# Pairing the sample batches in the indexer and attention part of a hybrid-layer decode kernel

## The chip, the cores and the metric

The kernel runs on one core of a Trainium2 chip. The metric is device microseconds of one execution, as the median of three runs.

## The reference

One layer of a hybrid decoder: two mixers read the same input projection, and their outputs are merged. There are 256 prompt tokens and 8 sample sequences ("batches") of 8 new tokens, each with 1024 cached positions, so 320 tokens in all. Mixer A is a gated delta rule (GDN) with a matrix state per head. Mixer B is sparse attention: an indexer scores the keys, the best are selected, and attention runs over those. The sample part of mixer B, which the change touches, computes:

```python
kidx_all = concatenate([cache_kidx[page_table], kidx])                 # 1024 + 8 keys per batch
logits = einsum('bqhd,bkd->bqhk', qi, kidx_all) * IDX_DH ** -0.5       # 16 indexer heads
score = einsum('bqhk,bqh->bqk', relu(logits), wi) * IDX_HEADS ** -0.5
idx = top_k(score, 256)
s = einsum('bqngd,bqknd->bqngk', q, k_sel) * ATT_DH ** -0.5            # 2 KV heads, 8 query heads each
o = einsum('bqngk,bqknd->bqngd', softmax(s), v_sel)
```

Each of these products exists once per batch, with 8 tokens; all weights' products are over the 320 tokens together.

## The kernel before

A Python planner writes the whole program out once, in order. `Kernel.stream` (L387) is its spine: 480 units, each of which loads 512 KB of weights (`raw`), casts them on ScalarE (`whi`), subtracts on VectorE (`wlo`), and multiplies with 24 main matmuls of 128 weight columns against the 320 tokens (16 of `whi` with the high and low parts of the tokens, 8 of `wlo`). Casts and differences are written two units ahead. After the 12th and the 24th matmul of a unit `side_round` (L305) lets every waiting side generator take one step, if the planner's clock says that its operands are ready (`ready`, `until`, `need`, `idle`). Matmuls of the generators so stand between main matmuls; a few generators must come first for the stream to go on, and then `force` (L329) runs side rounds with no main matmul between them. Below, "main count" is the number of main matmuls that stand ahead of a place in TensorE's queue.

Side generators that the change or its effects touch:

- `aux_gen` (L1114): products of the small columns (index weights, decay and beta), among the first side work.
- `sample_branch` (L1411): for one batch after another it gathers the indexer keys (`a8` tiles, 1024 + 1024 columns: as gathered and transposed in 32 by 32 blocks on VectorE), multiplies them with the queries `qiS` (16 matmuls in four row groups, one PSUM bank each, with 256 of the bank's 512 columns used), applies the relu, and in the next turn sums over heads with `wsel` (4 matmuls and one of 8 columns for the new keys). The queries come back from DRAM per batch into two slots (`fill`, L1388). The rows go to `scs`, where 32 rounds on VectorE select the best. `gate_gen` (L862) shares the `a8` ring.
- Its second half is the attention: per batch a gather of K and one of V (1 MB each), 32 by 32 transposes of K on VectorE, a visit with the mask products (`bs`, `esel`) and the scores (`qS`), reductions and five exponentials, a visit with 36 transposes of the probabilities (`tr4`, L242), and a visit with the value sums. `sample_out` (L1610) turns a batch's output and multiplies it with the gate.
- GDN, from main count 3744: `v_done` (L1795) takes a `vf` tile for each value block and forces side rounds until one is free. A tile becomes free in `v_gen` (L2055), when the value block is turned, and a `vt` tile to turn it into is free only after `prompt_chain` (L2086) and `sample_chain` (L2163) of an earlier head pair have finished. Before these stands `inverse` (L1938), the triangular inverse of the chunks, in parts.

Side products use six PSUM banks (`ps`), main ones two (`pm`). Helpers record every operation, so all rows of the profile carry line L64.

## Time and profile before

| | us |
|---|---|
| median of three runs (2122.76 to 2122.95) | 2122.89 |
| the profiled execution, its own time | 2128.34 |
| its span, first to last instruction | 2126.6 |
| TensorE busy in the span | 2093.1 |
| VectorE busy | 1416.3 |
| ScalarE busy | 985.3 |
| GpSimd busy | 464.0 |

The clock that TensorE was granted is 0.998 of full speed over the span. In a timeline each row has the start, the length, the engine, the operation with its output and inputs, and the count of instructions that the row groups; a bracket gives the idle time ahead of it and what ended it. TensorE's matmuls of four-byte numbers leave two records each. Lengths overlap, so what a piece of work takes on TensorE is read from start to start.

### The profile page before, as it was taken

How to read it: one execution, taken by the hardware profiler on the slowest of the kernel's cores; microseconds unless marked ns; L12 is line 12 of the kernel's file. 1: busy time of each engine (PE TensorE's matmuls, PEld its weight loads, DVE VectorE, ACT ScalarE, POOL GpSimd, SP SyncE). 2: the span in 40 equal slices, each digit the busy share in tenths (PEclk: the TensorE clock that was granted, in tenths of full speed). 3: DMA queues.
4: the chain of work that ended last, by engine and by line, in shares of the span. 5: the costliest groups of instructions: out<-in, count | busy, mean ns of one | idle time of the engine just before them, and what ended most of it. 6: DMA issues, size and time to landing. Idle time of an engine off the chain costs nothing.

```text
span 2126.6 us, 45305 instructions
## 1 busy us (share of the span) xinstructions
PE 2093.1 (98%) x17769; PEld 2020.2 (95%) x17769; DVE 1416.3 (67%) x2898; ACT 985.3 (46%) x2253; POOL 464.0 (22%) x661
## 2 busy tenths in 40 slices
PE   7999999999999999999999999999999999999997
PEld 7999989999999999899999999999999999999997
DVE  4776647889855477777878786868665545455543
ACT  3224473333344455465646464656545534333343
POOL 1001000000010108361818181818080000000000
PEclk9999999999999999999999999999999999999999
DMA  9996659776578667686868686868687867555562
GB/s 344 333 337 184 177 140 261 224 210 197 167 239 247 202 186 203 160 233 181 228 173 232 173 232 171 234 170 229 171 245 214 247 204 211 169 154 150 163 181 81
DMA packets 713989, 438.99 MB, mean 206 GB/s; under 512 B 73936, under 2 KB 697136, under 8 KB 711472
## 3 DMA queue, kind: packets, MB, share of 16 engines
q1 hardware_dynamic: 709696, 413.45, 68.3%
q0 software_dynamic: 3616, 21.02, 3.0%
q8 instruction: 139, 2.28, 0.5%
q10 hardware_dynamic: 464, 1.65, 0.2%
q14 instruction: 74, 0.61, 0.1%
HBM read 386.81 MB, written 48.94 MB: 205 GB/s over the span
## 4 chain that ended last, share of the span: by engine, by line
PE 70%; issue 22%; DVE 3%; DMA 2%; ACT 2%; SPq 0%; DVEq 0%; POOL 0%; POOLq 0%; ACTq 0%
PE pm L64 54%; PE ps L64 16%; DVE S L64 1%; DVE wlo L64 1%; DMA rawx<-in_w_ada_dram 1%; DMA a<-in_w_ada_dram 1%; DMA out_dram<-s 0%; DVE ps L64 0%; ACT whi L64 0%; DMA qiS<-d_qi 0%; ACT ot L64 0%; SPq L64 0%; DMA c<-in_c_sample_dram 0%; ACT s L64 0%; DMA cst<-in_state_conv_dram 0%
## 5 line engine op out<-in xcount | busy, mean ns | idle before, releaser
L64 PE MATMUL pm<-xh,whi 128*128 128x320 f32 (+1 forms) x3108 | 942.5, 317 | 2.7 <-DVE qiS L64 1.3
L64 PE MATMUL pm<-xl,whi 128*128 128x320 f32 (+1 forms) x3108 | 910.2, 307 | 0.3 <-DVE xl L64 0.2
L64 DVE TENSOR_TENSOR wlo<-raw,whi 128x1024 fp32r<-128x1024 f32 x466 | 576.8, 1247 | 245.8 <-ACT whi L64 233.7
L64 PEld LDWEIGHTS pm<-xh,whi 128*128 128x128 f32 x3108 | 584.2, 188 | 27.9 <-issue 20.2
L64 PEld LDWEIGHTS pm<-xl,whi 128*128 128x128 f32 x3108 | 585.0, 188 | 1.6 <-DVE xl L64 0.7
L64 ACT ACTIVATE whi<-raw 128x1024 fp32r<-128x1024 f32 x466 | 488.5, 1058 | 168.1 <-PE pm L64 103.8
L64 PE MATMUL pm<-xh,wlo 128*128 128x320 f32 (+1 forms) x3108 | 521.3, 307 | 0.5 <-DVE wlo L64 0.5
L64 PEld LDWEIGHTS pm<-xh,wlo 128*128 128x128 f32 x3108 | 469.4, 188 | 0.9 <-DVE wlo L64 0.9
L64 POOL TENSOR_TENSOR X<-X,tmpx 48x31 f32<-48x31 f32 (+15 forms) x248 | 175.5, 708 | 19.4
L64 POOL TENSOR_TENSOR tmpx<-blk,X 48x31 f32<-48x31 f32 (+15 forms) x248 | 162.0, 653 | 53.0 <-DMA blk<-d_b 34.8
L64 DVE SCALAR_TENSOR_TENSOR ps<-xp,cs,ps 128x344 f32<-128x344 f32 x192 | 111.5, 581 | 6.8
L64 POOL TENSOR_TENSOR sc<-sc,mh 128x6 f32<-128x6 f32 (+1 forms) x24 | 44.3, 1848 | 285.4 <-DVE sc L64 206.0
L64 PE MATMUL pm<-y1h,whi 128*128 128x320 f32 x336 | 99.5, 309 | 1.8 <-DVE M L64 0.9
L64 POOL TENSOR_TENSOR rfin<-rfin,mh 128x3 f32<-128x3 f32 x1 | 0.8, 848 | 455.5 <-DVE rfin L64 455.5
L64 PE MATMUL pm<-y1l,whi 128*128 128x320 f32 x336 | 99.1, 307 | 0.0
L64 DVE SCALAR_TENSOR_TENSOR S<-S,gtr,ps 128x128 f32<-128x128 f32 x256 | 67.4, 342 | 0.1
L64 PEld LDWEIGHTS pm<-y1h,whi 128*128 128x128 f32 x336 | 62.8, 187 | 2.3 <-ACT whi L64 2.3
L64 PE MATMUL ps<-xh,whi 128*128 128x320 f32 (+1 forms) x220 | 64.7, 309 | 0.0
L64 ACT ACTIVATE xp<-pm 128x256 f32<-128x256 f32 (+1 forms) x128 | 32.0, 304 | 70.5 <-PE pm L64 70.5
L64 ACT ACTIVATE ot<-ot,sc 128x128 f32<-128x128 f32 x96 | 29.9, 390 | 73.5 <-DVE sc L64 73.5
L64 PE MATMUL ps<-xl,whi 128*128 128x320 f32 (+1 forms) x220 | 63.7, 304 | 0.0
L64 PEld LDWEIGHTS pm<-y1l,whi 128*128 128x128 f32 x336 | 63.1, 188 | 0.0
(403 smaller groups left out, 2793.3 us busy)
## 6 DMA issues: line engine op xcount, KB each, us to landing
raw<-in_w_in_dram SPq DMA_DIRECT2D x328, 512.0 KB
raw<-in_w_pa_dram SPq DMA_DIRECT2D x64, 512.0 KB
rawx<-in_w_ada_dram SPq DMA_DIRECT2D x18, 1024.0 KB
a<-in_w_ada_dram SPq DMA_DIRECT2D x16, 1024.0 KB
S<-in_state_gdn_dram SPq DMA_DIRECT2D x32, 512.0 KB
out_dram<-S SPq DMA_DIRECT2D x32, 512.0 KB
raw<-in_w_pb_dram SPq DMA_DIRECT2D x32, 512.0 KB
raw<-in_w_out_dram SPq DMA_DIRECT2D x32, 512.0 KB
```

Of the source, the lines that this page charges most:

```text
L64: made = fn(*args, **kw)
```

## The change

The sample branch handles batches in pairs. Two batches' scores share a PSUM bank (256 columns each), in the indexer and in the attention; the head sums of two batches stand together, with `wsel` padded from 8 to 32 columns so that a whole 32-row group is copied out at once; the sums for the new keys are made once for all eight batches (`put_own`). In the attention the transposes of two batches stand in one visit (64 small ones and one of 128 by 128 for the own scores), and so do the value sums of two batches. The eight tiles of a ring that is no longer used become a fourth `a8` tile, and the five `s` tiles the transposed probabilities. K and V of the first batches are asked for at round 24 of the selection if the gate generator has finished. New waits stand ahead of the matmuls of `aux_gen`, and some `ready` times have 1.5 or 2.0 us added.

```diff
+        self.flags.add("gate")
...
-        self.q_r = Ring([a.tile([128, NP], F32, name=f"q{j}") for j in range(EARLY)])
+        self.qall = a.tile([128, EARLY * NP], F32, name="qall")
+        self.q_r = Ring([self.qall[:, NP * j:NP * j + NP] for j in range(EARLY)])
...
-        self.wsel = a.tile([128, NB, TS], F32, name="wsel")
+        self.wsel = a.tile([128, NB, 32], F32, name="wsel")
...
-        self.s_r = Ring([a.tile([128, 384], F32, name=f"s{j}") for j in range(5)])
+        self.sall = a.tile([128, 2048], F32, name="sall")
+        self.s_r = Ring([self.sall[:, 384 * j:384 * j + 384] for j in range(5)])
...
-        self.a4 = Ring([a.tile([128, 9, 128], F32, name=f"a4{j}") for j in range(2)])
-        self.st = Ring([a.tile([128, 8], F32, name=f"st{j}") for j in range(6)])
+        self.a4 = Ring([a.tile([128, 2, 1024], F32, name="a4")])
+        self.st = Ring([a.tile([128, 16], F32, name=f"st{j}") for j in range(6)])
+        self.own2 = a.tile([128, 256], F32, name="own2")
+        self.own, self.ownT = self.own2[:, 0:128], self.own2[:, 128:256]
+        self.vSo = a.tile([128, 256], F32, name="vSo")
...
     def aux_gen(self):
         nc, a, i = self.nc, self.ap, self.i
         ax = self.auxf
+        yield self.ready(ax)
+        yield from self.need(self.ps_side)
...
-        yield
+        yield self.ready(g, rb)
+        yield from self.need(self.ps_side, 2)
...
-        yield
+        yield self.ready(self.G)
+        yield from self.need(self.ps_side)
...
+            self.nc.sync.dma_start(self.vSo[64:128, 128 * n:128 * n + 128], self.vS[0:64, 128 * n:128 * n + 128])
...
+        def turned(b):
+            yield from self.until(self.ready(raws[b][:, 0:1024]) + 1.5)
+            turn(raws[b][:, 1024:2048], raws[b][:, 0:1024])
...
-        for b in range(NB + 1):
-            yield from self.need(self.ps_side, (4 if b < NB else 0) + (b > 0))
...
+        for b in range(0, NB + 2, 2):
+            while b > 2 and not {f"s{b - 4}", f"s{b - 3}"} <= self.flags:
+                yield
+            yield from self.need(self.ps_side, (4 if b < NB else 0) + (b > 0) + (b == 2))
             if b > 0:
-                yield from self.need(self.s_r)
+                if b == 2:
+                    yield from self.need(self.s_r)
                 p = self.psum()
-                for g in range(4):
-                    self.mm(p[32 * g:32 * g + 8, 0:256], self.wsel[:, b - 1, :],
-                            last.rearrange("p a b -> p (a b)")[:, 256 * g:256 * g + 256], skip=True)
-                self.mm(p[0:8, 256:264], self.wsel[:, b - 1, :], self.newi[:, b - 1, :], skip=True)
+                for e in range(2):
+                    for g in range(4):
+                        self.mm(p[32 * g:32 * g + 32, 256 * e:256 * e + 256], self.wsel[:, b - 2 + e, :],
+                                last[:, e, 256 * g:256 * g + 256], skip=True)
+                if b == 2:
+                    pn = self.psum()
+                    for c in range(NB):
+                        self.mm(pn[0:32, 8 * c:8 * c + 8], self.wsel[:, c, :], self.newi[:, c, :], skip=True)
                 self.a4.put(last)
             if b < NB:
                 last = self.a4.get()
-                rl = last.rearrange("p a b -> p (a b)")
                 ps = [self.psum() for _ in range(4)]
-                kt = raws[b][:, 1024:2048].rearrange("p (e j c) -> p j e c", e=8, j=4)
-                q = self.slot(self.qiS, b)
-                for j in range(4):
-                    for g in range(4):
-                        r = slice(32 * g, 32 * g + 32)
-                        self.mm(ps[g][:, 0:256].rearrange("p (e c) -> p e c", e=8), q[r, j, :], kt[r, j],
-                                start=(j == 0), stop=(j == 3), skip=True)
+                for e in range(2):
+                    kt = raws[b + e][:, 1024:2048].rearrange("p (e j c) -> p j e c", e=8, j=4)
+                    q = self.slot(self.qiS, b + e)
+                    for j in range(4):
+                        for g in range(4):
+                            r = slice(32 * g, 32 * g + 32)
+                            self.mm(ps[g][:, 256 * e:256 * e + 256].rearrange("p (e c) -> p e c", e=8), q[r, j, :], kt[r, j],
+                                    start=(j == 0), stop=(j == 3), skip=True)
                 for g in range(4):
-                    self.act(rl[:, 256 * g:256 * g + 256], ps[g][:, 0:256], AF.Relu, scale=SC)
+                    self.act(last[:, :, 256 * g:256 * g + 256], ps[g].rearrange("p (e c) -> p e c", e=2), AF.Relu, scale=SC)
                     self.ps_side.put(ps[g])
-                self.a8.put(raws.pop(b))
+                for e in range(2):
+                    self.a8.put(raws.pop(b + e))
             if b > 0:
+                for e in range(2):
+                    sb = sums[e]
+                    self.act(sb.rearrange("r (c e) -> r e c", e=8),
+                             p[:, 256 * e:256 * e + 256].rearrange("r (e c) -> r e c", e=8))
+                    self.spawn(put_scores(b - 2 + e, sb))
+                self.ps_side.put(p)
+            if b == 2:
                 sb = self.s_r.get()
-                for g in range(4):
-                    r = slice(32 * g, 32 * g + 8)
-                    self.act(sb[r, 0:256].rearrange("r (c e) -> r e c", e=8),
-                             p[r, 0:256].rearrange("r (e c) -> r e c", e=8))
-                self.act(sb[0:8, 248 + 8 * b:256 + 8 * b], p[0:8, 256:264])
-                self.ps_side.put(p)
-                self.spawn(put_scores(b - 1, sb))
-            if b + 3 < NB:
-                yield from fetch(b + 3)
-            if b + 1 < NB:
-                yield from self.until(self.ready(raws[b + 1]))
-                turn(raws[b + 1][:, 1024:2048], raws[b + 1][:, 0:1024])
+                self.act(sb[0:32, 0:64], pn[0:32, 0:64])
+                self.ps_side.put(pn)
+                self.spawn(put_own(sb))
+            yield from fetch(b + 3)
+            yield from fetch(b + 4)
             if b + 2 < NB:
-                yield self.idle(self.slot(self.qiS, b))
-                self.fill(self.qiS, self.d_qi, b + 2)
-            if b + 1 < NB:
-                yield from self.until(self.ready(raws[b + 1], self.slot(self.qiS, b + 1), last))
+                yield from turned(b + 2)
+                yield self.idle(self.qiS[:, 0:8])
+                for e in range(2):
+                    self.fill(self.qiS, self.d_qi, b + 2 + e)
+                yield from turned(b + 3)
+                yield max(self.ready(raws[b + 2], raws[b + 3], last), self.ready(self.qiS[:, 0:8]) + 2.0)
...
+            if it == 24 and "gate" in self.flags:
+                for b in range(2):
+                    yield from load(K, ck, b)
+                yield from load(V, cv, 0)
...
+            yield from self.until(self.ready(K[b]) + 1.5)
...
+        self.q_r.free.clear()
+        self.s_r.free.clear()
+        self.a8.put(self.qall)
+        yield from load(V, cv, 1)
+        pT = self.sall.rearrange("p (k r) -> p k r", r=128)
+        own, ownT = self.own, self.ownT
+        vown = self.vS, self.vSo
+        width = (256, 256, 256, 256, 64)
+        order = (4, 0, 1, 2, 3)
+        for b in range(0, NB, 2):
+            yield self.ready(K[b], K[b + 1], self.bs, self.qS)
...
-            ktv = K[b].rearrange("p (e n j c) -> p n j e c", e=8, n=2, j=4)
-            qr = self.slot(self.qS, b)
-            es = self.esel[:, b % 4].rearrange("p h t -> p (h t)")
-            width = (256, 256, 256, 256, 64)
-            for g, (p, w) in enumerate(zip(ps, width)):
-                k, c = (slice(32 * g, 32 * g + 32), 0) if g < 4 else (slice(0, 32), 256)
-                self.mm(p[:, 0:w], es[k], self.bs[k, b // 4, c:c + w], start=True, stop=True)
...
+            for e in range(2):
+                es = self.esel[:, (b + e) % 4].rearrange("p h t -> p (h t)")
+                for g, (p, w) in enumerate(zip(ps, width)):
+                    k, c = (slice(32 * g, 32 * g + 32), 0) if g < 4 else (slice(0, 32), 256)
+                    self.mm(p[:, w * e:w * e + w], es[k], self.bs[k, (b + e) // 4, c:c + w], start=(e == 0), stop=True,
+                            skip=True)
...
             for g in order:
-                nc.vector.tensor_reduce(st[:, g:g + 1], ps[g][:, 0:width[g]], axis=AX.X, op=OP.max)
-            nc.vector.tensor_reduce(st[:, 5:6], st[:, 0:5], axis=AX.X, op=OP.max, negate=True)
...
+                nc.vector.tensor_reduce(sv[:, :, g], ps[g][:, 0:2 * width[g]].rearrange("p (e c) -> p e c", e=2), axis=AX.X,
+                                        op=OP.max)
+            nc.vector.tensor_reduce(sv[:, :, 5], sv[:, :, 0:5], axis=AX.X, op=OP.max, negate=True)
...
+                    if e == 1:
+                        self.ps_side.put(ps[g])
+                if e == 0:
+                    yield
...
+            if b + 2 < NB:
+                for e in range(2):
+                    yield from load(K, ck, b + 2 + e)
             yield then
...
-            yield self.ready(pT, V[b])
+                for e in range(2):
+                    self.fill(self.qS, self.d_q, b + 2 + e)
+            yield from self.need(self.ps_side, 5)
+            ps, p = [self.psum() for _ in range(4)], self.psum()
+            for e in range(2):
+                for k in range(8):
+                    self.tr4(ps, 8 * e + k, pr[:, e, 128 * k:128 * k + 128])
+            self.tr(p[:, 0:128], own)
+            self.act(ownT, p[:, 0:128])
+            self.ps_side.put(p)
+            self.out4(ps, 16, pT.rearrange("p k r -> p (k r)"))
+            then = self.ready(pT, ownT, V[b], V[b + 1])
+            if b + 2 < NB:
+                yield from k_trans(b + 2)
+            yield then
...
+            for e in range(2):
+                for k in range(9):
+                    for n in range(2):
+                        c, h = 128 * n, slice(64 * n, 64 * n + 64)
+                        l = pT[:, 8 * e + k, h] if k < 8 else ownT[:, h]
+                        r = V[b + e][:, 256 * k + c:256 * k + c + 128] if k < 8 else vown[e][:, c:c + 128]
+                        self.mm(p[h, 128 * e:128 * e + 128], l, r, start=(k == 0), stop=(k == 8), skip=True)
...
+            self.spawn(self.sample_out(b, pr, st))
             if b + 2 < NB:
+                for e in range(2):
+                    yield from load(V, cv, b + 2 + e)
+                yield from k_trans(b + 3)
```

What this does to TensorE's queue in the attention: before, value sums of one batch (`a` transposed probabilities against a V tile, `vS` for the new tokens) are followed in the same visit by the next batch's mask products and scores:

```order
L64 MATMUL pm_66<-xh,whi_80 128x320
L64 MATMUL pm_66<-xl,whi_80 128x320
L64 MATMUL ps_68<-a_2258,a_2261 64x128 x16
L64 MATMUL ps_68<-vS,a_2261 64x128 x2
L64 LDWEIGHTS esel
L64 MATMUL ps_69<-bs,esel 128x256
```

After, the value sums of two batches stand by themselves; `sall` is the tile of the transposed probabilities, `qall` the fourth gather tile:

```order
L64 MATMUL pm_65<-xl,whi_78 128x320
L64 MATMUL pm_65<-xh,wlo_81 128x320 x8
L64 MATMUL ps_67<-a_2248,sall 64x128 x16
L64 MATMUL ps_67<-vS,own_2256 64x128 x2
L64 MATMUL ps_67<-qall,sall 64x128 x16
L64 MATMUL ps_67<-vSo,own_2256 64x128 x2
L64 MATMUL pm_65<-xh,whi_79 128x320
```

The joined visit is gone: per pair there is a visit of 74 score matmuls, 84 main matmuls later one of 65 transposes, and 36 later one of 36 value sums.

The planner's clock sees other times, and so places further down move too. In the first GDN head pair the `inverse` starts at main count 4632 where it started at 4584, and the forced rounds of the value block at 4704 are seven where there was one. VectorE before, at that place (`S` is the states of one head over the sample batches, `w` and `vt` the chains' operands, `ot` and `PT` outputs and products):

```order
L64 SCALAR_TENSOR_TENSOR S_8000<-S_8000,gtr,ps_72 128x128 x4
L64 SCALAR_TENSOR_TENSOR S_8000<-S_8000,gtr,ps_70 128x128 x4
L64 TENSOR_TENSOR wlo_82<-raw_75,whi_79 128x1024
L64 TENSOR_SCALAR w_7991<-ps_69,sc_8002 128x128 x2
L64 SCALAR_TENSOR_TENSOR vf_7970<-cth_7954,ps_71 128x256
L64 SCALAR_TENSOR_TENSOR vf_7970<-cth_7954,ps_71 128x8x8
L64 TENSOR_SCALAR w_7996<-ps_67,sc_8002 128x128 x2
L64 TENSOR_TENSOR wlo_83<-raw_75,whi_80 128x1024
L64 SCALAR_TENSOR_TENSOR vt_7990<-ps_72,neG,vt_7990 128x128 x2
L64 SCALAR_TENSOR_TENSOR w_7992<-w_7992,gtp,ps_68 128x128 x2
L64 TENSOR_TENSOR ot_7997<-ps_68,ot_7997 128x256
L64 SCALAR_TENSOR_TENSOR S_8001<-S_8001,gtr,ps_70 128x128 x4
```

VectorE after, at that place:

```order
L64 SCALAR_TENSOR_TENSOR vt_7856<-ps_67,neG,vt_7856 128x128 x2
L64 SCALAR_TENSOR_TENSOR vt_7855<-ps_69,neG,vt_7855 128x128 x2
L64 SCALAR_TENSOR_TENSOR S_7866<-S_7866,gtr,ps_70 128x128 x4
L64 SCALAR_TENSOR_TENSOR S_7866<-S_7866,gtr,ps_72 128x128 x4
L64 SCALAR_TENSOR_TENSOR S_7866<-S_7866,gtr,ps_71 128x128 x4
L64 SCALAR_TENSOR_TENSOR S_7866<-S_7866,gtr,ps_67 128x128 x4
L64 TENSOR_SCALAR w_7862<-ps_70,sc_7868 128x128 x2
L64 TENSOR_SCALAR w_7857<-ps_69,sc_7868 128x128 x2
L64 SCALAR_TENSOR_TENSOR vt_7856<-ps_72,neG,vt_7856 128x128 x2
L64 SCALAR_TENSOR_TENSOR S_7867<-S_7867,gtr,ps_71 128x128 x4
L64 SCALAR_TENSOR_TENSOR S_7867<-S_7867,gtr,ps_67 128x128 x4
L64 SCALAR_TENSOR_TENSOR S_7867<-S_7867,gtr,ps_70 128x128 x4
```

Before, two `wlo` of the stream and a value block stand between the two sets of updates of `S`, and TensorE has main matmuls in its queue there. After, only steps of the chains stand between them. On TensorE the chains' matmuls stood in eight visits between 4644 and 4764; after, 55 of them stand in one visit at 4704, which begins with

```order
L64 MATMUL pm_65<-xh,wlo_81 128x320 x8
L64 MATMUL ps_70<-w_7857,ktok_7832 128x256
L64 MATMUL ps_70<-vt_7855,PT_7847 128x128 x2
L64 MATMUL ps_72<-vt_7855,XT_7852 128x128 x2
L64 MATMUL ps_71<-vt_7856,XT_7852 128x128 x2
L64 MATMUL ps_67<-S_7867,R_7829 32x256 x8
L64 MATMUL ps_69<-w_7858,kq_7824 128x256 x2
L64 MATMUL ps_70<-w_7859,ktok_7832 128x256
```

where each chain's row needs that chain's row before it. From main count 7788 on TensorE's order is as before.

More of the change, by code (lines that the diff above doesn't have):

```diff
@@ L1027, in attention @@
                                          base=0, channel_multiplier=1)
-        for t in self.a4.free:
-            self.nc.gpsimd.memset(t[0:8, 2:4, :], 0.0)
         self.aux_setup()
@@ L1492, in sample_branch @@
+            yield from fetch(b + 3)
+            yield from fetch(b + 4)
+            if b + 2 < NB:
+                yield from turned(b + 2)
[4 more added lines that the diff above has]
+                yield max(self.ready(raws[b + 2], raws[b + 3], last), self.ready(self.qiS[:, 0:8]) + 2.0)
             elif b < NB:
                 yield self.ready(last)
-        while f"s{NB - 1}" not in self.flags:
+        while not {f"s{b}" for b in range(NB)} | {"own"} <= self.flags:
@@ L1504, in sample_branch, with load @@
         yield from self.need(self.st)
-        m8 = self.st.get()
+        st = self.st.get()
+        m8 = st[:, 0:8]
+        K, V = {}, {}
+        def load(to, cache, b):
+            yield from self.need(self.a8)
+            to[b] = self.a8.get()
+            self.gather(to[b], cache, b)
         for it in range(32):
@@ L1574, in sample_branch @@
-            nc.vector.tensor_reduce(st[:, 6:7], st[:, 0:5], axis=AX.X, op=OP.add)
-            nc.vector.reciprocal(st[:, 7:8], st[:, 6:7])
-            self.a8.put(K.pop(b))
-            then = self.ready(pr)
-            if b + 1 < NB:
-                yield from load(V, cv, b + 1)
-                yield from self.until(self.ready(K[b + 1]))
-                k_trans(b + 1)
+            for e in range(2):
[4 more added lines that the diff above has]
+                            skip=True)
@@ L1582, in sample_branch @@
+            nc.vector.tensor_reduce(sv[:, :, 6], sv[:, :, 0:5], axis=AX.X, op=OP.add)
+            nc.vector.reciprocal(sv[:, :, 7], sv[:, :, 6])
+            then = self.ready(pr, own)
+            for e in range(2):
+                self.a8.put(K.pop(b + e))
+            if b + 2 < NB:
+                for e in range(2):
+                    yield from load(K, ck, b + 2 + e)
             yield then
             if b + 2 < NB:
-                self.fill(self.qS, self.d_q, b + 2)
-            yield from self.need(self.a4)
@@ L1593, in sample_branch @@
+            for e in range(2):
+                for k in range(8):
[8 more added lines that the diff above has]
+            yield then
             yield from self.need(self.ps_side)
```

158 lines of the change are left out of this document (77 added, 81 removed).

## The prediction

> **What bounds the kernel now.** I read the page's busy times first, then a table by stage, then what TensorE waits for in the stages that the change touches, and last the timeline of single visits there.
>
> ```profile
> PE 2093.1 (98%) x17769; PEld 2020.2 (95%) x17769; DVE 1416.3 (67%) x2898; ACT 985.3 (46%) x2253; POOL 464.0 (22%) x661
> 570.00:720.00 150.00, 150.00 (x1797) 139.03 (x1796) 85.19 (x161) 59.60 (x145) 13.80 (x26) 1.00 0.76 228
> ```
>
> TensorE is busy for 98% of the span, and for all 150 us of the sample attention (570 to 720); the first three columns of pairs after the window are TensorE, its weight loads and VectorE. So the end of the program moves only by what TensorE's queue holds and by what it waits for. VectorE at 57% and ScalarE at 40% of that stage have room: work that they lose is worth nothing by itself. Of waits there is little:
>
> ```profile
> PE ps L64 <- DMA qiS<-d_qi: 1.0, 2, 0.8
> PE ps L64 <- ACT s L64: 1.2, 1, 1.2
> PE ps L64 <- DVE auxf L64: 0.5, 1, 0.5
> ```
>
> I call a run of side matmuls between two main matmuls a visit. Four views of TensorE's timeline price them (columns: start, length, what, count of records; a four-byte matmul leaves two records). First the indexer scores:
>
> ```profile
> 276.72 0.62 PE L64 MATMUL ps<-a,wsel 128*8 128x256 f32 x8
> ...
> 279.22 0.41 PE L64 MATMUL pm<-xh,whi 128*128 128x320 f32 x1
> 279.47 0.31 PE L64 MATMUL pm<-xl,whi 128*128 128x320 f32 x1
> ...
> 280.94 0.31 PE L64 MATMUL pm<-xl,whi 128*128 128x320 f32 x1
> 281.18 0.62 PE L64 MATMUL ps<-a,wsel 128*8 128x256 f32 x8
> ...
> 286.01 0.41 PE L64 MATMUL pm<-xh,whi 128*128 128x320 f32 x1
> ```
>
> Main matmuls start 0.147 us apart (ten steps from 279.47 to 280.94). Around a tiled visit it is 0.24 before the first side matmul (280.94 to 281.18) and 0.25 after the first main one (279.22 to 279.47): 0.09 and 0.10 too much, each visit. The first visit shown takes 2.50 us, the second, with the same matmuls, 4.83: its transfer of queries was late (the qiS wait above), which cost 2.33, more than the 1.0 that the waits list.
>
> **The change part by part.** The profiled execution took 2128.34 us (span 2126.6 and 1.74 around it), 5.45 above the median 2122.89 of the three timed runs; I work out differences in the profiled execution and apply them to the median, since the terms lie far inside the span.
>
> *Scores in pairs.* Nine visits become five, with the same score and sum matmuls (the columns padded from 8 to 32 add no matmul). What a visit costs beside its matmuls also has an end part, which the attention's first visit shows (its last 16 of the 64 records stand apart):
>
> ```profile
> 582.58 0.31 PE L64 MATMUL ps<-bs,esel 32*128 32x256 bf16 x5
> 582.81 1.98 PE L64 MATMUL ps<-a,qS 32*64 32x256 f32 x64
> ...
> 584.16 0.64 PE L64 MATMUL ps<-a,qS 32*64 32x256 f32 x16
> 584.73 0.42 PE L64 MATMUL pm<-xh,whi 128*128 128x320 f32 x1
> ```
>
> From 582.81 to 584.16, 48 records take 1.35, so 16 take 0.45; the last 16 take 0.57 until the main matmul, so the tail is 0.12, with the start's own delay some 0.15. A visit saved is worth 0.09 + 0.10 + 0.15 = 0.34, and four of them 1.4. The late query transfer (2.33) should go in the main: a batch's queries were asked for when the batch two before it had been scored, 24 main matmuls and a visit (6.0 us) ahead; a pair's are asked for 48 or 60 (7.1 or 8.8 us) ahead, and the plan now adds 2.0 us to its idea of their arrival. But there are twice as many at once, and the scores also wait for two gathers of indexer keys and their transposes, which start when key tiles come free after the scores; no row prices two, so I charge 0.9 (0 to 4.6: twice the late one). Scores: −1.4 − 2.3 + 0.9 = −2.8.
>
> *Attention in pairs.* The other visits that carry it now:
>
> ```profile
> 590.20 0.75 PE L64 MATMUL ps<-ident,a 32*128 32x32 f32 x36
> 590.88 0.42 PE L64 MATMUL pm<-xh,whi 128*128 128x320 f32 x1
> ...
> 600.48 2.33 PE L64 MATMUL ps<-a,qS 32*64 32x256 f32 x64
> ...
> 714.59 1.98 PE L64 MATMUL ps<-a,qS 32*64 32x256 f32 x64
> ...
> 728.25 1.97 PE L64 MATMUL ps<-a,a 128*64 128x128 f32 x32
> ...
> 730.37 0.42 PE L64 MATMUL pm<-xh,whi 128*128 128x320 f32 x1
> ```
>
> Before, value sums of one batch and scores of the next share a visit. Values take 2.12 (728.25 to 730.37), scores 2.15 (582.58 to 584.73). In six of the seven joined visits the score records run 2.33 (600.48) and not 1.98 (582.81, and 714.59 in the last joined visit): 0.35 more, 2.50 in all. In all: 6 × 4.62 + 4.27 + 2.15 + 2.12 + 8 × 0.68 for the transposes = 41.7, and 17 visits × 0.19 = 3.2: 44.9 us. After, for each pair: scores 2 × 2.15 − 0.15 + 0.19 = 4.3; values 2 × 2.12 − 0.15 + 0.19 = 4.3; transposes, 64 records instead of 72, 64/36 × 0.53 (0.68 less the tail) + 0.15 + 0.19, and a full transpose of the own scores at about 0.25, 1.5. That is 10.1, and 40.5 for four pairs: −4.4. If the paired scores run in the longer way it is 0.35 per visit back, so −3.0; I take −4.0. The Trainium skill says in "TensorEngine Tiling (Array Packing)", Key Properties, that changing the tiling mode drains TensorE. By that rule alone, with 12 changes of form per two batches before and 8 after and half of 0.34 for each, the sum would be −2.7; the 0.35 in six joined visits is no drain at a change, as the seventh has the same changes without it.
>
> What the pairs ask of the others, by the rows of one batch:
>
> ```profile
> 584.80 1.42 DVE L64 TENSOR_REDUCE st<-ps 128x1 f32<-128x256 f32 x4 [1.45 <-PE ps L64]
> 586.25 0.16 DVE L64 TENSOR_REDUCE st<-st 128x1 f32<-128x5 f32 x1
> 588.71 0.16 DVE L64 TENSOR_REDUCE st<-st 128x1 f32<-128x5 f32 x1 [2.29 <-ACT a L64]
> ```
>
> VectorE reduces for 1.42 and then waits 2.29 for five exponentials. For a pair that is about 3.2 of reductions (the short ones with them) and 4.4 of exponentials, 7.6 us, and the transposes come 84 main matmuls, 12.3 us, after the scores. The fewer instructions on VectorE and ScalarE, and the single evacuations, are hidden and cost nothing; the freed tiles (a fourth gather tile) let K come earlier and are needed by nothing on TensorE now. SyncE gets two more transfers (the second batch's own values) and asks for two batches' queries at once; the weight blocks behind these in its queue are cast two blocks, 7 us, before they are used, so this costs 0; without that cover a late block would show as TensorE waits on whi.
>
> *The aux products.* The new waits ahead of them keep TensorE's queue free of matmuls whose input isn't there: the waits on auxf (0.5) and s (1.2) go: −1.6, since what is queued behind is main work that is ready. At worst (nothing to hide the aux results) 0.
>
> *The GDN start.* The order of the first GDN head pair changes, as a side effect: the chunk inverse comes 48 main matmuls later, and what followed it in eight visits now stands in one of 55 matmuls, since the next value block needs a tile that this chain must first release. Its rows before:
>
> ```profile
> 899.68 0.59 PE L64 MATMUL ps<-w,ktok 128*128 128x256 f32 x2
> ...
> 902.99 0.44 PE L64 MATMUL ps<-ident,vf 128*128 128x128 f32 x2 [0.53 <-DVE S L64]
> 904.03 0.66 PE L64 MATMUL ps<-ident,vf 128*128 128x128 f32 x4 [0.60 <-DVE S L64]
> 904.44 0.39 PE L64 MATMUL pm<-xh,whi 128*128 128x320 f32 x1
> ```
>
> ```profile
> 901.82 4.22 DVE L64 SCALAR_TENSOR_TENSOR S<-S,gtr,ps 128x128 f32<-128x128 f32 x16
> ```
>
> A set of 16 state updates holds VectorE for 4.22 us, 0.26 each (so 0.55 for two vector steps of that size), and the banks that TensorE wants next. The visit from 899.68 holds 32 records in 4.76, 3.6 without its two waits of 1.1 on that set: 0.11 a record, and some 12 us for the 110 records of the 55 matmuls. Now both sets stand in this visit. By the order, some 40 records lead to the first set, so that it begins at about 4.5 us; until it ends at 8.7 the operand behind it on VectorE (0.55) isn't there, and TensorE has matmuls until about 7.8: 1.5 lost. Two such steps later the second set runs from about 10.5 to 14.7, and the last transposes wait for its banks: 2.2 more. That is 3.7 against 1.1: +2.6, as an estimate. If every vector step in the visit were exposed (8.4 for the sets and 11 pairs at 0.55 behind the matmuls, less the 1.1) it would be +13.4; if the sets hid wholly, −1.1.
>
> Add +0.5 for new small waits at other places where the order shifts (0 to 2). Sum: −2.8 − 4.0 − 1.6 + 2.6 + 0.5 = −5.3, and 2122.9 − 5.3 = **2117.6**.
>
> **The rivals.** *The GDN visit eats the gain.* Half-way between the estimate and full exposure, +8.0 in place of +2.6, gives 2123.0: no change. For it: each step of the chains takes the one before it by data, from TensorE to VectorE and back. Against: main work in front has its weights split two blocks ahead, and the matmuls of one chain lie beside the vector steps of the other.
>
> *The exponentials come too late (slower).* Place: the transposes of each pair. ScalarE and VectorE also serve the stream, by the groups of the whole run:
>
> ```profile
> L64 DVE TENSOR_TENSOR wlo<-raw,whi 128x1024 fp32r<-128x1024 f32 x466 | 576.8, 1247 | 245.8 <-ACT whi L64 233.7
> L64 ACT ACTIVATE whi<-raw 128x1024 fp32r<-128x1024 f32 x466 | 488.5, 1058 | 168.1 <-PE pm L64 103.8
> ```
>
> In 12.3 us stand 3.5 blocks. If all their casts (3.7) and differences (4.4) go ahead of the pair's 7.6, the last exponential ends at 15.7 and TensorE waits 3.4 us at each of four pairs: +13.6, 2131.2. It makes the kernel slower from 2.4 us per pair on (2127.1 less 2117.6, by four). Against: the two engines' stream work runs partly side by side, which brings the end to about 12. The Trainium skill speaks for it: "PSUM — Partial Sum Buffer", section on PSUM bank collisions, has no two engines in one bank and quadrant at a time, so a bank shared by two batches is given back only after both. The trace agrees as far as all five exponentials lie between the short reductions at 586.25 and 588.71, but shows no shared bank.
>
> *The pairs save nothing.* If a visit's price goes with its matmuls, −2.8 and −4.0 shrink to −1.4 (the late queries) and −1.4 (the longer scores half gone), and the sum to −1.3: 2121.6, no change.
>
> *More than forecast.* The GDN visit costs nothing and no gather is late: 2122.9 − 3.7 − 4.0 − 1.6 + 0.5 = 2114.1.
>
> **How the numbers follow.** Forecast 0.47, GDN rival 0.23, late exponentials 0.13, nothing saved 0.07, more than forecast 0.10. A difference of 0.2% (4.2 us) is about what a measurement of this kernel can tell: faster is below 2118.6, slower above 2127.1. Faster holds the forecast and the last case, 0.57; same 0.30; slower 0.13. The range takes in the last case with a little for −4.4 in the attention and no loss elsewhere, the late queries met again, and the GDN rival: 2112.5 to 2124.0.
>
> **What would show it.** Right: five score visits, the full one at about 4.6 us, none with a qiS wait; value visits of 4.2 us; no waits on auxf and s; one long visit near 900 us of about 15 us, with waits on S of 3 to 4. Wrong: waits on DMA of the indexer keys or on their transposes around 280, waits on ACT at the attention's transposes, S or w waits over 6 us near 900, or paired visits as long as two single ones.

## The result: 0.6% slower, and the profile after

| | before | after |
|---|---|---|
| median of the timed runs, same chip | 2122.82 (2121.45 to 2122.95) | 2134.72 (2133.94 to 2135.4) |
| the profiled execution, its own time | 2128.34 | 2134.91 |
| its span | 2126.6 | 2133.2 |

The ratio is 1.0057, with a 95% interval of 1.004 to 1.0075: 11.9 us slower, where 5.3 us faster was forecast. The page's first row shows no engine that became the bound:

```profile
PE 2089.9 (98%) x17741; PEld 2021.9 (95%) x17741; DVE 1419.2 (67%) x2858; ACT 968.4 (45%) x2202; POOL 464.1 (22%) x654
```

TensorE is busy 3.2 us less than before, and the span is 6.6 us longer. So work was saved, and waiting was added. (These 6.6 are less than the 11.9 of the medians, since the profiled execution of the kernel before took 5.5 us more than its median.) To see where, I laid the two profiles over each other by main count: how long after the start does the n-th main matmul begin? At 4500 the changed kernel is 13.5 us ahead (841.77 against 855.24); at 7800 it is 7.2 behind (1484.05 against 1476.86); from there to the end the distance is constant within 0.5. What the profile loses, it loses in the GDN stage.

First the parts that were meant to gain. A full visit of indexer scores, in TensorE's timeline (side matmuls leave two records each here, the main ones, whose operands are rounded to `fp32r`, one):

```profile
306.07 1.07 PE L64 MATMUL ps<-a,wsel 128*32 128x256 f32 x16
307.08 3.73 PE L64 MATMUL ps<-a,qiS 32*128 32x256 f32 x64
310.74 0.41 PE L64 MATMUL pm<-xh,whi 128*128 128x320 f32 x1
```

It takes 4.67 from its first matmul to the next main one, and none of the five visits has a wait on `qiS`. The three visits of an attention pair:

```profile
580.26 1.19 PE L64 MATMUL ps<-ident,a 32*128 32x32 f32 x64
581.38 0.33 PE L64 MATMUL ps<-ident,own 128*128 128x128 f32 x1
581.47 0.39 PE L64 MATMUL pm<-xh,whi 128*128 128x320 f32 x1
...
586.91 1.97 PE L64 MATMUL ps<-a,sall 128*64 128x128 f32 x32
588.71 0.39 PE L64 MATMUL ps<-vS,own 128*64 128x128 f32 x4
...
591.00 0.42 PE L64 MATMUL pm<-xh,whi 128*128 128x320 f32 x1
...
596.68 0.45 PE L64 MATMUL ps<-bs,esel 32*128 32x256 bf16 x10
597.06 3.71 PE L64 MATMUL ps<-a,qS 32*64 32x256 f32 x128
...
600.70 0.41 PE L64 MATMUL pm<-xh,whi 128*128 128x320 f32 x1
```

Transposes take 1.21, value sums 4.09 and scores 4.02, each start to start. No row has a bracket: the transposes never wait for the exponentials.

Then the long visit of the GDN start, and VectorE's two sets of state updates in it:

```profile
878.40 0.59 PE L64 MATMUL ps<-w,ktok 128*128 128x256 f32 x2
...
888.40 2.27 PE L64 MATMUL ps<-w,ktok 32*128 32x256 f32 x18 [1.12 <-DVE w L64]
...
893.95 0.66 PE L64 MATMUL ps<-ident,vf 128*128 128x128 f32 x4 [0.59 <-DVE S L64]
894.36 0.39 PE L64 MATMUL pm<-xh,whi 128*128 128x320 f32 x1
```

```profile
883.62 4.21 DVE L64 SCALAR_TENSOR_TENSOR S<-S,gtr,ps 128x128 f32<-128x128 f32 x16
889.67 4.22 DVE L64 SCALAR_TENSOR_TENSOR S<-S,gtr,ps 128x128 f32<-128x128 f32 x16 [0.29 <-PE ps L64]
```

The visit takes 15.96, and between the main counts 4500 and 4800 the changed kernel loses 2.9. That is the forecast's size (2.6), in part by luck: the waits in the visit come to 2.9, but only 1.2 of them are on `S`, where 3 to 4 were forecast; 1.1 is on `w`, and the rest on `vt` and `ot`. Up to 4800 the mechanisms are those of the prediction, and the changed kernel is 10.6 us ahead. What stands behind it was not predicted. What TensorE waits for between the main counts 4500 and 7800, the three longest rows:

```profile
PE pm L64 <- ACT whi L64: 8.8, 5, 4.4
PE ps L64 <- DMA cst<-in_conv_w_dram: 2.1, 2, 1.9
PE pm L64 <- DVE wlo L64: 1.9, 2, 1.7
```

The first and the third are waits of the stream itself, for weights that ScalarE and VectorE prepare. The longest, in the timeline of TensorE:

```profile
956.34 0.63 PE L64 MATMUL pm<-xh,whi 128*128 128x320 f32 x1 [4.41 <-ACT whi L64]
956.78 0.47 PE L64 MATMUL pm<-xl,whi 128*128 128x320 f32 x1
957.04 0.47 PE L64 MATMUL pm<-xh,whi 128*128 128x320 f32 x1
```

After the wait a main matmul takes 0.267 a step instead of 0.147, until 960.78. The windows (length; busy time of TensorE, its weight loads, VectorE, ScalarE and GpSimd; then the granted clock, here 0.80, 0.52 and 1.00) show the same:

```profile
951.00:956.00 5.00, 0.94 (x7) 0.67 (x5) 0.66 (x2) 4.05 (x16) 0.30 (x1) 0.80 0.88 268
956.00:961.00 5.00, 4.66 (x18) 4.66 (x19) 3.96 (x4) 3.79 (x7) 1.65 (x1) 0.52 0.67 184
961.00:966.00 5.00, 5.00 (x97) 4.50 (x96) 0.67 (x2) 2.89 (x7) 0.00 (x0) 1.00 1.12 330
```

So a wait of 4.4 costs about 2.0 more behind it. The Trainium skill ("TensorE: Matmul & The Clock Gate", The HAM clock gate) has the array's clock halved after an idle window of about 3.4 us. The trace does not agree in this: TensorE stopped at 951.93, and the clock was halved at 953.96, 2.0 us later. The last section shows what the traces have in its place.

What did ScalarE do ahead of 956? Its timeline, and that of SyncE's queue (x4 is four transfers in a row):

```profile
941.60 1.06 ACT L64 ACTIVATE whi<-raw 128x1024 fp32r<-128x1024 f32 x1
951.83 0.53 ACT L64 ACTIVATE zf<-pm,gh 128x320 f32<-128x320 f32 x1 [9.17 <-issue]
952.25 0.43 ACT L64 ACTIVATE cth<-pm 128x320 f32<-128x320 f32 x1
...
955.25 1.99 ACT L64 ACTIVATE whi<-raw 128x1024 fp32r<-128x1024 f32 x2
```

```profile
938.51 2.60 SPq L64 DMA_DIRECT2D blk<-d_o  x4
...
946.23 0.47 SPq L64 DMA_DIRECT2D X<-d_x  x1
946.80 0.39 SPq L64 DMA_DIRECT2D raw<-in_w_in_dram  x1
947.29 0.52 SPq L64 DMA_DIRECT2D d_ya<-zf  x1
```

ScalarE stands still for 9.17 us ahead of `zf<-pm`, and the two casts that TensorE wants stand behind that. The product in `pm` was finished by 943.5; what `zf` needed, the profile does not name ("issue"). SyncE's row gives the suspicion: the inverse's 15 transfers hold its queue from 938.51 to 946.70, and behind them stands the store of the tile that `zf` is about to overwrite. The trace's record of semaphores (the marks by which a transfer tells that it has landed) bears it out: the last of the 16 marks of the store issued at 947.29 came at 951.75, 0.08 us ahead of ScalarE's step.

### The profile page after: what moved, and what is told of

Read it like the earlier page. It is cut to its first block, busy times and chain, and to the rows that moved or that the text cites. A ratio compares the mean times of both kernels' runs of the same rounds, so it can differ in the third digit from the quotient of the medians.

```text
span 2133.2 us, 45095 instructions
## 1 busy us (share of the span) xinstructions
PE 2089.9 (98%) x17741; PEld 2021.9 (95%) x17741; DVE 1419.2 (67%) x2858; ACT 968.4 (45%) x2202; POOL 464.1 (22%) x654
## 4 chain that ended last, share of the span: by engine, by line
PE 64%; issue 22%; DVE 5%; ACT 3%; DMA 3%; SPq 1%; POOL 1%; DVEq 0%; POOLq 0%; ACTq 0%
PE pm L64 49%; PE ps L64 14%; DVE S L64 2%; SPq L64 1%; DVE wlo L64 1%; DMA raw<-in_w_ada_dram 1%; ACT whi L64 1%; DVE ps L64 1%; ACT ot L64 1%; ACT ps L64 1%; DMA rawx<-in_w_ada_dram 1%; POOL X L64 0%; ACT vt L64 0%; POOL tmpx L64 0%; DVE w L64 0%
## 5 line engine op out<-in xcount | busy, mean ns | idle before, releaser
L64 DVE TENSOR_TENSOR wlo<-raw,whi 128x1024 fp32r<-128x1024 f32 x466 | 586.7, 1267 | 258.7 <-ACT whi L64 242.2
L64 POOL TENSOR_TENSOR X<-X,tmpx 48x31 f32<-48x31 f32 (+15 forms) x248 | 182.1, 734 | 19.4
L64 POOL DMA_INDIRECT a<-in_cache_k_dram,idx x8 | 7.5, 936 | 280.2 <-PE ps L64 265.3
```

The costliest lines, as they stand in the source:

```text
L64: made = fn(*args, **kw)
```

## The experiments

Two theories at first. **Order**: the pairs gain what they should, and the new order of the GDN stage, which the planner chose because its clock stood elsewhere when the stage opened, loses it again. **Profiler** and **pairs**: the loss is not real outside the profiled execution, or it comes from what the pairs do to tiles and queues. The order can be set apart from the pairs: one line at the opening of GDN gives the planner another idea of how long the transfers asked for so far will take, and it then writes the stage out in the other of the two orders, the same on all five queues to the end of the program. (The traces of e1_pin and of the kernel before have the same operations in the same sequence on every engine and in SyncE's queue from main count 3900 on; so have those of e2_flip and the changed kernel.)

**e1_pin**: the pairs, with the old GDN order.

```diff
     def gdn_open(self):
+        self.clock.t["dma"] = self.clock.t["tensor"] + 8.0
```

> The changed kernel with one line in gdn_open that moves the planner's own idea of the DMA queue's backlog. No instruction changes; from the first GDN unit on, every engine's order is that of the kernel before, and ahead of it that of the changed kernel. Theory (the order): the pairs gain in their own stage what was forecast (2.8 + 4.0 + 1.6 = 8.4) and the whole loss is the GDN order that the changed plan falls into, so 2122.8 - 8.4 = 2114.4, within 2112 to 2117. Rival 1 (part of the gain is only there under the profiler, whose execution of the kernel before is 5.4 above its timed median): 2119 to 2121. Rival 2 (the pairs themselves disturb what comes after, by the transfers or the earlier arrival, whatever the order): 2128 to 2135.

Measured: 2114.27 (2112.94 to 2115.61), ratio to the kernel before on that chip 0.9938 (0.9924 to 0.9951). This is the fastest kernel of the study, ahead of both. That the median falls on the expected 2114.4 is chance: the kernel before took 2128.17 on that chip and not 2122.8, so the gain is 13.9 us, where 8.4 was expected. In the GDN stage TensorE then waits for one thing only, in two places:

```profile
PE ps L64 <- DVE S L64: 1.1, 2, 0.6
```

**e2_flip**: the kernel before, with the new GDN order.

```diff
     def gdn_open(self):
+        self.clock.t["dma"] = self.clock.t["tensor"] + 2.3
```

> The kernel before with the same line set the other way: its sample part unchanged, and from the first GDN unit on the order of the changed kernel on every engine. Theory (the order): the loss is all there without the pairs, 2134.7 + 8.4 = 2143, with the long visit near 900 us and ScalarE's late casts in it as in the changed kernel. Rival 1 (profiler): the order costs 12 + 3 = 15, so about 2138. Rival 2 (the pairs disturb): 2122 to 2126.

Measured: 2157.1 (2155.53 to 2160.5), ratio 1.0142 (1.0126 to 1.0157). The loss comes without any pair, and larger than expected (2143 against 2122.8 would be 1.0095). From main count 4500 to 7800 it takes 644.1 against 622.0 in e4_before, 22.1 more; 7.9 more were lost before 4500, of which some 5 lie behind main count 3744, where GDN begins: there TensorE waits 3.29 at 752.31 for the convolution's state (`cst`), with a window of half clock behind it, where the changed kernel waits 0.35 at the same main count. Why that transfer is late in one and not in the other stays open.

**e4_before**: the kernel before as it is, for a second profile.

> The kernel before once more, for a second profile. Its first profiled execution took 5.4 us more than its timed runs. If that is chance, a second profile is 2122 to 2125 and lacks some of the waits of the first (the late queries near 284 us, 2.3, above all). If the profiler itself makes this kernel slower, it is again about 2128 with the same waits.

Measured: 2126.59, span 2124.9, beside 2128.17 (2123.94 to 2130.16) for its timed runs on that chip. That lies between the two expected cases. The late queries were there again (a visit of 4.15), the wait on `s` was shorter (0.45 where it was 1.17). The profiler does not make this kernel slower: the profiled execution is below the median. The kernel's executions differ by some us by themselves, and in the four comparisons of this study its medians lie between 2122.8 and 2128.2. Below, times are compared on one chip only, and ratios to the kernel before on the same chip otherwise.

**e3_noaux**: e1_pin without the new waits ahead of the aux products.

```diff
     def aux_gen(self):
-        yield self.ready(ax)
-        yield from self.need(self.ps_side)
...
-        yield self.ready(g, rb)
-        yield from self.need(self.ps_side, 2)
+        yield
...
-        yield self.ready(self.G)
-        yield from self.need(self.ps_side)
+        yield
```

> The kernel of e1_pin with the waits ahead of the aux products taken out again, so those matmuls stand in TensorE's queue before their inputs are there; the GDN order stays that of the kernel before. By the forecast the waits on auxf and on s come back and cost 1.6: 1.6 above e1_pin, 0 to 2.4. A rival: other work slips in and it costs nothing, within 0.5 of e1_pin.

Measured: 2117.21 (2115.02 to 2120.65), ratio 0.9953 (0.994 to 0.9967). By the medians the waits are worth 2.9 us, by the profiles at main count 4500 2.0; the two intervals of the ratios overlap, so the size is rough.

So the order is the cause. What in it? By main counts 4500 to 7800 the two orders differ by 22.4 us (642.28 changed, 619.84 e1_pin), of which 13.4 are seven waits (one of 1.1 within the long visit) and 3.6 the slow steps behind two of them. Of the other 5.4, 1.8 lie in the long visit; the rest was not taken apart. Theory **A**, in two halves: (1) the wait near 956 comes through SyncE's queue, as read above. (2) The shorter ones at 1128, 1145 and 1366 come through VectorE's queue:

```profile
1125.54 1.87 ACT L64 ACTIVATE ot<-ot,sc 128x128 f32<-128x128 f32 x6 [5.23 <-DVE sc L64]
1127.31 1.99 ACT L64 ACTIVATE whi<-raw 128x1024 fp32r<-128x1024 f32 x2
```

```profile
1118.46 4.21 DVE L64 SCALAR_TENSOR_TENSOR S<-S,gtr,ps 128x128 f32<-128x128 f32 x16
...
1123.30 1.81 DVE L64 SCALAR_TENSOR_TENSOR ps<-xp,cs,ps 128x344 f32<-128x344 f32 x3
1125.02 0.48 DVE L64 TENSOR_TENSOR sc<-sc,sc 128x6 f32<-128x6 f32 x1
```

ScalarE's scaling of `ot` waits 5.23 us for a product of six columns, which stands in VectorE's queue behind 16 state updates and a convolution; two casts stand behind the scaling. Such waits alone are not what tells the orders apart. In the changed kernel's stage they come to 52.9 us in 12 waits; in e1_pin's:

```profile
ACT ot L64 <- DVE sc L64: 59.9, 12, 5.4
```

There ScalarE waits for this product longer in all, and yet TensorE waits for no cast. That the difference lies in which casts stand behind such a wait, and how soon they are needed, is read from the rows; no run changes that alone.

The rivals: **B**, ScalarE has too much to do there, whatever it waits for; **C**, a wait that is removed comes back at the next place; **D**, the edits gain by themselves, in any order. For these runs the order was kept word for word on TensorE and ScalarE; only the named instruction changes its queue. (`placed` issues an instruction on one queue and enters it in the planner's clock on the other, so that the plan stays as it was.)

**f0_after**: the changed kernel again.

> The changed kernel again, as the yardstick of the three below on the same chip. All theories: about 2134.7 (2133 to 2137), with the waits of the first execution again: TensorE on whi 4.4 us near 956, and 1.2 to 2.0 us at five more places.

Measured: 2135.93 (2134.66 to 2138.65), ratio 1.0055 (1.0038 to 1.0072). The seven waits stand in the same places and are as long within 0.1 us but for one (the conv weights, 2.63 instead of 1.92).

**f1_store**: the stores of the finished heads on GpSimd's queue.

```diff
+    def placed(self, real, planned, op, *args, **kw):
+        getattr(getattr(self.tc.nc, real), op)(*args, **kw)
+        self.clock.enter(planned, op, args, kw)
...
-            nc.sync.dma_start(self.d_ya[hv + v], y)
+            self.placed("gpsimd", "sync", "dma_start", self.d_ya[hv + v], y)
```

> Same order on TensorE, ScalarE and VectorE; only the 32 stores of the finished heads (d_ya) are issued on GpSimd's queue instead of SyncE's. Theory A (the long wait near 956 comes from the SyncE queue: 15 transfers of the inverse stand ahead of a store, the store holds a zf tile, ScalarE's next step needs that tile, and two casts stand behind it): the 4.4 us wait goes, and with it 2.4 us of slower clock behind it, so 6.8 us less than the changed kernel, about 2128. Rival B (ScalarE is held there by TensorE's own block, or the weights themselves arrive late behind those transfers): the wait stays within 1 us of 4.4, and the time within 1.5 us of the changed kernel's.

Measured: 2135.96 (2132.25 to 2139.13), ratio 1.0048 (1.0032 to 1.0065). At the place theory A holds to the tenth: the wait near 956 is gone, and the profile is 6.7 us shorter between main counts 5000 and 5100. The step of ScalarE that stood still for 9.17 us now waits for its product alone, and for 0.91:

```profile
948.73 0.53 ACT L64 ACTIVATE zf<-pm,gh 128x320 f32<-128x320 f32 x1 [0.91 <-PE pm L64]
```

The total doesn't show it; by the total alone rival B's number came. In the profiled execution 5.1 us were lost at main counts 900 to 1000, ahead of every edited instruction, and 4.2 near 8900 (a wait of 3.20 for `M`, and half clock behind it). The first is a wait that comes and goes: 4.16 here (for `qall`, by ScalarE), 2.03 in g1_early, 3.01 in g3_pin, and under 0.7 in the other profiles of kernels with the pairs. Four executions that spread over 7 us can't settle 7 us; f3 and g2 do.

**f2_prod**: the small product on GpSimd, at the place in the program where it stood.

```diff
-        self.tt(mv(12), mv(12), qf, OP.mult)
+        self.emitted += 1
+        self.placed("gpsimd", "vector", "tensor_tensor", mv(12), mv(12), qf, OP.mult)
```

> Same order on TensorE, ScalarE and SyncE; only the last small product of each head's norm factor (6 columns, 16 in all) moves from VectorE's queue to GpSimd's. Theory A (at 1128, 1145 and 1366 casts stand behind ScalarE's scaling of ot, which waits 5 to 6 us for that product, which stands in VectorE's queue behind a convolution and two weight differences): the three waits of 1.7, 1.2 and 1.3 us go, with the slow steps behind them 4.5 us less than the changed kernel (3 to 6), about 2130. Rival B (casts are late because ScalarE has too much to do there, whatever it waits for): less than 1.5 us gained.

Measured: 2142.43 (2137.48 to 2144.16), ratio 1.0082 (1.0063 to 1.0102): slower. Neither theory had that. The wait had only changed its queue (ScalarE's waits in that stage):

```profile
ACT ot L64 <- POOL sc L223: 52.4, 10, 8.9
```

In the changed kernel it is 52.9 in 12 waits, with VectorE named. On GpSimd, for nine of the stage's twelve heads, eight instructions of an inverse stand between the power and the product, and they take 5.3 to 8.0 us. The cast wait near 1128 went, but cast waits of 1.6 (near 929) and 1.7 (1031) came new, the one of 1.2 near 1145 became 3.0, and the one near 1366 stayed (1.41). The edit was the wrong test of a right reading.

**f3_both**: f1 and f2.

> Both edits. Theory A: the gains add, 10 to 12 us less than the changed kernel, about 2124, and what then stays over the kernel with the old order (2114) is the longer visit and the waits on wlo near 922 and on conv weights near 1370, some 9 us. Rival B: within 3 us of the changed kernel. Rival C (a wait that is removed comes back at the next place, since the blocks are only shifted): f3 gains less than the larger of the two alone.

Measured: 2133.96 (2133.2 to 2135.22), ratio 1.0047 (1.003 to 1.0064). It is 8.5 us faster than f2_prod by the medians, so the store is worth its 6.8 in the time as well; f2's harm stays. The total by itself is what rivals B and C said (2.0 below f0_after), so it decides nothing between the theories; the step from f2_prod does.

**g1_early**: the product on GpSimd, directly behind the power.

```diff
         self.tt(m[:, 12:18], m[:, 6:12], self.mh.to_broadcast([128, 6]), OP.pow, eng=nc.gpsimd)
+        self.tc.nc.gpsimd.tensor_tensor(mv(12), mv(12), qf, OP.mult)
         yield
-        self.tt(mv(12), mv(12), qf, OP.mult)
+        self.emitted += 1
+        self.clock.enter("vector", "tensor_tensor", (mv(12), mv(12), qf, OP.mult), {})
```

> The changed kernel's order on TensorE, ScalarE and SyncE; the last small product of each head's norm factor stands on GpSimd directly behind the power that it needs, with no step of the inverse in between. Theory A (casts stand behind ScalarE's scaling of ot, and the scaling waits for this product in VectorE's queue): ScalarE's wait for the factor is cut, and the waits of 1.7, 1.2 and 1.3 us at 1128, 1145 and 1366 go; with slow steps behind them about 5 us less than the changed kernel (2135.9 on the last chip), and up to 2 more where the scaling near 911 starts earlier. Rival B (ScalarE's work itself is too much there): under 1.5 us gained. The 4.4 us wait near 956 stays in both.

Measured: 2130.49 (2128.84 to 2132.94), ratio 1.0023 (1.0014 to 1.0032). Against f0_after's 1.0055 that is some 6.8 us gained, in the stage 8.0. ScalarE's waits for the factor fall from 52.9 to 9.8:

```profile
ACT ot L64 <- POOL sc L2321: 9.8, 5, 4.2
```

The waits at 1128, 1145 and 1366 are gone, and 0.26 is left of the one near 922; the one near 956 stays (4.77). B is out: ScalarE does the same work in the same order. C holds at one place: behind the wait near 1366 the one for the conv weights grew to 3.81.

**g2_both**: g1 and f1.

> The early product and the stores on GpSimd's queue. Theory A: the waits near 956, 1128, 1145 and 1366 all go, 11 to 13 us less than the changed kernel (ratio to the kernel before 0.9995, 0.998 to 1.001), and the stage of the main counts 4500 to 8000 is within 10 us of the kernel with the old order instead of 22. Rival C (removed waits come back elsewhere): at least 5 us more than that.

Measured: 2124.32 (2122.37 to 2127.98), ratio 0.9997 (0.9987 to 1.0006), where 0.9995 was expected. The stage from main count 4500 to 7800, in windows, for f0_after, g2_both and e1_pin:

```profile
842.45:1486.14 643.69, 626.68 (x5087) 598.21 (x5086) 489.45 (x1159) 361.02 (x1006) 302.44 (x418) 0.99 0.74 196
```

```profile
844.26:1472.92 628.66, 622.12 (x5087) 595.66 (x5086) 488.81 (x1151) 362.68 (x1006) 325.89 (x453) 1.00 0.76 201
```

```profile
842.76:1462.60 619.84, 618.72 (x5087) 593.73 (x5086) 483.24 (x1156) 359.77 (x1006) 297.77 (x412) 1.00 0.76 203
```

15.0 us of 23.9 are back, with the same instructions on TensorE and ScalarE. Of the 8.8 that stay, TensorE's waits show these two and the long visit's:

```profile
PE ps L64 <- DMA cst<-in_conv_w_dram: 3.2, 1, 3.2
PE ps L64 <- DVE S L64: 1.2, 3, 0.6
PE ps L64 <- DVE w L64: 1.1, 1, 1.1
```

The wait for the conv weights, with slow steps behind it, and the long visit (2.9) make up most; no run takes these two away. C is out as a whole. But the 1.32 near 1366 came back in the wait for the conv weights behind it, so at that place little was gained.

**g3_pin**: both edits in e1_pin.

> Both edits in the kernel with the pairs and the old GDN order, where TensorE has no wait over 0.9 us in that stage. Theory A: nothing to gain there, ratio to the kernel before 0.994 as without them (0.9925 to 0.9955). If the edits are good by themselves, whatever the order (rival D: they remove ScalarE work or DMA load and not those waits), it gains as much here as in the other order, ratio about 0.989.

Measured: 2120.39 (2117.97 to 2123.04), ratio 0.9973 (0.9964 to 0.9982). It does not gain, so D is out. It isn't the same either, as A expected, but some 7 us slower than e1_pin by the ratios. The profile has 4.8 of it in the stage (624.6 against 619.8), where a cast wait of 2.1 us appears near 946, and 4.3 at main counts 900 to 1000, the wait that comes and goes. The wait near 946 is the same chain through the other queue:

```profile
943.91 0.53 ACT L64 ACTIVATE zf<-pm,gh 128x320 f32<-128x320 f32 x1 [5.67 <-DMA d_ya<-zf]
```

In this order the store, on GpSimd's queue, stands behind the instructions of an inverse, the last of them a copy from 937.56 to 939.66; ScalarE waits 5.67 us for the tile, where in e1_pin the same step waits for nothing, and two casts stand behind. So GpSimd's queue is no better place for these instructions; it was better in the one order in which they were waited for. The Trainium skill ("Perfetto Trace Analysis", DMA Optimizations) suggests that input and output transfers be given to different issuing engines; f1_store agrees at the place where a store stood in the way, and g3_pin, with both edits, shows a loss where none did.

## Why the prediction was wrong

**The step that failed** is "+0.5 for new small waits at other places where the order shifts (0 to 2)". It took the cost of the new order outside the long visit as next to nothing, and it measured some 18 us: from main count 4500 to 7800 the changed kernel takes 642.3 against 621.6 before, 20.7 more, of which the long visit, forecast by itself, is 2.9. I followed the changed order where TensorE's own rows differed most, at the one long visit, and priced only that. The other four queues had changed over the same 3300 main matmuls, and there I asked only whether each engine was busy enough to matter. By that ask no engine was: ScalarE is busy 45% of the span. But what counts is what a cast stands behind in its queue, and what that waits for. e1_pin and e2_flip show that the order costs this, with the pairs and without them; f1_store, g1_early and g2_both show for 15.0 us of it that it comes through two instructions for which ScalarE waits.

**The cover named for the casts** ("the weight blocks ... are cast two blocks, 7 us, before they are used, so this costs 0") fails with it. It was argued for SyncE's new transfers in the sample stage, where it held; in the GDN stage ScalarE stands still for 9.17 us, longer than the cover.

**The terms that were forecast.** Scores: nine visits of 23.2 us in all, with the 0.09 ahead of each, became five of 19.6, −3.6 (forecast −2.8; the charge of 0.9 for late gathers did not occur). Attention: 43.7 became 38.9, −4.8 (−4.0; all paired scores run in the short form here, 4.0 a visit, so the worked-out −4.4 was nearer; that is no property of the pairs, as three of the four take 4.73 in e1_pin; −2.7, by the rule on tiling modes, is refuted as a total). Aux: −2.0 to −2.9 by e3_noaux, after the fact (−1.6); the wait on `auxf` went, of the one on `s`, now `sall`, 0.63 is left. At main count 4500 the profile is 13.5 us ahead where these terms said 8.4; a wait of 0.7 near 330 went and one of 1.0 near 179 became 0.4, and two profiles of the kernel before differ by 2.1 there (855.24 and 853.10). The GDN visit: +2.9 (+2.6), with other waits in it than forecast. Two sums of the working are 0.1 off: the six joined visits take 4.64 each on average and not 4.62, and the waits on `auxf` and `s` make 1.7.

**The rivals.** The exponentials were never late; pairs did save; the GDN visit did not eat the gain. The time fell outside the range, above every case: all four looked at the sample stage or at the one visit. A rival "the planner's other order exposes the casts", priced by the waits that one late cast can cause, was missing. "Wrong" signs were named near 280, at the attention's transposes and near 900; the true one, TensorE waiting on `whi`, was named for late weight blocks alone.

## What to carry to other kernels

Where a planner writes the order, a change in one stage changes the others through the planner's clock: price every queue of the shifted stage, or fix the order downstream and price the edit alone; here that was worth 22 us, more than the edit itself (−13). Look for what a prefetch (here a cast) stands behind on its engine and what the instruction ahead of it waits for; an engine that is busy half the time can still hold it longer than its lead. A wait is not removed by moving it to another queue: f2_prod moved it and lost, g1_early put it where nothing stood ahead and won, and the store that gained 6.8 us in one order held ScalarE for 5.67 in the other.

## What was not expected of the hardware

- A wait can cost half as much again behind it. After 4.41 us without work 15 main matmuls ran at 0.267 us a step instead of 0.147. Near 1370 the same happened for 3.4 us behind a wait of only 1.92, and there are no slow steps behind the wait of 1.7 near 1128. The traces show why. From start to end of a profile the half clock begins on a grid of 3.413 us: in the changed kernel at 953.96 and 1370.39, 122 steps apart. Some windows of that grid (the bounds; length; TensorE's busy time; the clock; two columns of the DMA):

```profile
919.83:923.24 3.41, 1.71 (x12) 1.00 0.53 152
950.55:953.96 3.41, 1.39 (x10) 1.00 1.03 309
953.96:957.37 3.41, 1.03 (x4) 0.50 0.42 123
1124.63:1128.04 3.41, 2.06 (x15) 1.00 1.02 272
1366.98:1370.39 3.41, 1.49 (x12) 1.00 1.07 288
1370.39:1373.80 3.41, 3.41 (x15) 0.50 0.75 219
```

  Behind a window with 1.39 or 1.49 busy the next is at half clock; behind 1.71 or 2.06 it is not. In all 13 profiles, between 220 and 2000 us, the least idle time in a window that led from full to half clock is 1.92 us, and the most that did not is 1.81 (f3_both, 1364.70 to 1368.11). So in this stream what counts is how much of a wait falls into one window: the 1.7 near 1128 is cut by the grid, 1.35 in one window and 0.36 in the next. An idle window of 3.4 us, the rule cited above, is not needed. Idle time is not the whole measure either: windows that end at 206.53 in e2_flip and at 212.54 in g1_early had 1.53 and 0.77 idle and led to half clock too, with matmuls of 32 columns in them.
- Executions of the same kernel differ by up to 7 us here (2132.25 to 2139.13 for f1_store), partly through one early wait of 0 to 4.2 us at main counts 900 to 1000. What makes that wait long or short stays open.
